# Two transformer blocks on one core: the second block's layer 0 in three column chunks instead of two

## The chip, the cores and the metric

The kernel runs on one core of a Trainium2 chip. The metric is the device time of one execution in microseconds (us), as the median of several runs. All times below are in us unless ns is written.

## What is computed

Two transformer blocks run one after the other on 512 tokens of width 1024. The change touches only the second one. It has two layers. Each works on x (512 tokens) and, in layer 0, also on a context of 256 tokens that goes through the same weights:

```
h  = layer_norm(x) * (1 + sc1) + sh1          # modulate; the context has its own sh, sc, g
y  = mixing_sublayer(h, hc, ...)              # projections by w_in, three kinds of heads, w_o
x  = layer_norm(ALPHA * x + g1 * y) * ln1_g + ln1_b
x  = layer_norm(ALPHA * x + g2 * swiglu_2(modulate(x, sh2, sc2), w_ffn_in, w_ffn_out)) * ln2_g + ln2_b
```

`swiglu_2(h)` is `(silu(h @ a) * (h @ b)) @ w_ffn_out`. In layer 1 the context is only read for keys and values (projection units 16 and 17), and has no output.

## The kernel before, in words

All activations lie transposed: eight tiles X[j] of 128 features (partitions) by 768 columns, of which columns 0 to 511 are x and 512 to 767 the context. A weight is fetched in units of 128 output features (up to 1024 k-values a row, 512 KB). `wunit` (L279) loads a unit on SP's queue two to three units ahead (`wload`, L252) and splits it (`wsplit`, L261): ScalarE rounds it to `whi` (L269), VectorE takes the difference `wlo` (L271). Activations are split in the same way, `ah` and `al`. `linear` (L305) then issues three matmuls for every k-step and chunk of columns (`mm3`, L296: lines L300, L301, L303). A unit that serves several stretches of columns at different times is fetched and split again each time.

Layer 0 of the second block (`layer2`, L1193) ends in two stages that go part by part through the columns. `PARTS` (L41) lists the parts: (first column, width).

- **"wo" stage.** `wo` (L1209) multiplies the merged heads by w_o and adds into X. For part 0, five of eight units run as filling work beside the attention (k-steps 3 to 7), then three more units, then k-steps 0 to 2 of all eight. For each later part all eight units run with all eight k-steps. A group norm with its split, ("a", part), must be done before a part begins. After each part its norm work is queued: `norms1` (L1260) is a `postln` (L1167) and then a `modulate` (L1150), two layer norms in a row, a double norm below.
- **Feed-forward** (`ffn`, L487). Unit pairs f = 0 to 21, each with two input units. The first NSKEW = 4 pairs go part by part (skewed), so that they can begin when the first part's norm is done; the middle goes over all columns; of the last group NTAIL = 4 pairs and the eight output units (21 matmuls of a chunk, 448 KB) go part by part again. After the output units of a part `norms2` (L1280) is queued: postln, then the next layer's modulate into new tiles H3, then the spill of X.

Queued norm work (`later`, L201) is a list of Python generators, first in, first out. `pump` (L213) steps through it as matmul columns are issued: a step for each 2400 x pace columns. The pace is PN for norms1 and PL for norms2, and at most 0.5 while more than one generator waits. A double norm has some 60 steps. `need` (L237) runs the steps that are left before the work that depends on them. This sets the priority of instructions; a planner (the tile framework) orders each engine's instructions by it and by readiness, except GpSimd's (POOL), which keep the order of the program.

A layer norm (`ln`, L1103): POOL adds pairs of X tiles (L1125), TensorE averages them (L1131), VectorE subtracts the mean (L1136), ScalarE squares (L1137), POOL adds squares (L441), TensorE sums over features (L369), VectorE forms 1/sqrt (`rsqrt`) and a diagonal (L394), and TensorE broadcasts it (L407). Then postln scales (L1173, L1174), or modulate writes `ah` (L1162) and `al` (L1163). Pair sums, squares and modulate's intermediate take buffers of `sqtile`, three of them.

Activation tiles come from `hilo` (L483), eight buffers for `ah` and eight for `al`. The merged heads A and the feed-forward's input H2 are the same tiles; H3 is a new set of eight from the same buffers.

Layer 1 begins with `gqa` (L1530): its `run` (L1587) goes through projection units in an order that SKEW gives. Before, SKEW[1] takes units 16, 17, 11, 12, 9, 10 over columns 0 to 383, then over 384 to 767; units other than 16 and 17 stop at column 512, so they have 128 columns left in the second chunk. `run` waits for the norms of the parts (`hparts`) that overlap a chunk. After that, units 13, 14 and 15 fill the beginning of the attention.

Layer 1's own end uses two parts of 256 columns in both kernels, with six skewed pairs.

Of the kernel before, what the change touches and what calls it, by code (L numbers as in the profile page):

```python
# [37 lines left out]

PARTS = ((0, 384), (384, 384))  # L41
SKEW = (
    (((16, 17, 11, 12, 9, 10), ((0, 256), (512, 256)), ((256, 256),)),),
    (((16, 17, 11, 12, 9, 10), ((0, 384),), ((384, 384),)),),
)
NSKEW = (3, 4, 4, 6)
NTAIL = (0, 0, 4, 0)
# [18 lines left out]
LOOK = (1, 1)  # L66


PL = ((0.8, 0.6), (0.5, 0.5))
PN = ((0.5, 0.4), (0.5, 0.5))  # L70
PF = (0.5, 0.5)
PM = (0.5, 0.5)
P2 = (0.7, 0.7)
# [56 lines left out]
class Kern:  # L130
# [1062 lines left out]
    def layer2(self, l, H, skew):  # L1193
# [4 lines left out]
        T = S if last else T2  # L1198
        parts = ((0, 256), (256, 256)) if last else PARTS
        pool = lambda name, **kw: tc.tile_pool(name=f"{name}{l}", bufs=1, reuse_waits="tile", **kw)  # L1200
# [17 lines left out]
        with pool("o") as op:  # L1218
# [41 lines left out]
            def norms1(c0, n):  # L1260
                yield from self.postln(X, c0, n, f"ln1g{l}", f"ln1b{l}")
                yield from self.modulate(X, H2, c0, n, m, 3, 4)
# [6 lines left out]
            for h in range(len(parts)):  # L1269
                self.need(("a", h))  # L1270
                for _ in wo(range(KD), h, 0, 3 if h < nw else 8):
                    pass
                self.later(("n", h), norms1(*parts[h]), PN[l][h])
            self.need(("a", len(parts) - 1))
# [5 lines left out]
        def norms2(c0, n, cnt):  # L1280
            yield from self.postln(X, c0, n, f"ln2g{l}", f"ln2b{l}", cnt)
            if last:
                for j in range(KD):
                    nc.sync.dma_start(out=self.out[j][:, c0:c0 + n], in_=X[j][:, c0:c0 + n])
                return
            if not H3:
                H3.extend(self.hilo(T2))
            yield from self.modulate(X, H3, c0, n, self.mod[1], 0, 1)
            self.spill(X, c0, n)

        def after(h, cnt):
            self.later(("l", h), norms2(*parts[h], cnt), PL[l][h])

# [769 lines left out]
```

## Time and profile before

| what | us |
|---|---|
| median of 3 runs (lowest, highest) | 3386.17 (3385.2, 3391.33) |
| the profiled execution | 3387.66 |
| its span, first to last instruction | 3385.9 |
| TensorE matmul busy in it | 3223.0 (95%) |
| VectorE busy | 2076.3 (61%) |
| ScalarE busy | 1321.3 (39%) |
| GpSimd busy | 491.3 (15%) |

PE is TensorE's matmuls, PEld its weight loads, DVE VectorE, ACT ScalarE, POOL GpSimd, SP the queue that issues the weight loads. Matmuls overlap one another, so the time of one record is longer than the pace at which they follow; the pace is a window divided by its matmuls. PEclk is the granted TensorE clock, 1.0 for 2.4 GHz and 0.5 for 1.2 GHz. A wait is put down to the instruction that ended it.

### The profile page before, as it was taken

What the parts mean: (1) busy time and instruction counts of PE and PEld (TensorE: products, weight loads), DVE (VectorE), ACT (ScalarE), POOL (GpSimd) and SP (SyncE); (2) the same over time, 40 slices, a digit from 0 to 9 for tenths busy, and PEclk for the clock granted to TensorE, in tenths of its full rate; (3) what the DMA queues carried; (4) which work ended last, traced back from release to release, by engine and by line L of the source; (5) the groups of instructions that cost most, each with busy time, mean ns of one, the idle gap of its engine ahead of it and who ended that gap; (6) DMA issues with size and microseconds to landing.
All of it is one profiled execution on the core that took longest, in us unless ns stands there. A gap on an engine that the chain in (4) does not pass through costs nothing. (4 is left out here: it accounts for less than half of the span.)

```text
span 3385.9 us, 50242 instructions
## 1 busy us (share of the span) xinstructions
PE 3223.0 (95%) x19680; PEld 2875.9 (85%) x19680; DVE 2076.3 (61%) x4419; ACT 1321.3 (39%) x2273; POOL 491.3 (15%) x462
## 2 busy tenths in 40 slices
PE   8999999999999999999898989999999899889998
PEld 7999979988888987889787878888898787888887
DVE  7993568876633769856676764222257586773335
ACT  4222346653323423234464543111135365552223
POOL 0000023333200100012212240000013212320001
PEclk9999999999999999999999999999999799999999
DMA  6663431122223556644001322221234201343233
GB/s 208 210 213 95 123 97 45 54 70 64 66 94 101 191 177 192 216 123 143 19 27 53 92 75 90 66 63 56 69 118 136 74 27 53 118 126 112 89 98 107
DMA packets 112461, 351.22 MB, mean 104 GB/s; under 512 B 12960, under 2 KB 26912, under 8 KB 111968
## 3 DMA queue, kind: packets, MB, share of 16 engines
q1 hardware_dynamic: 86464, 280.07, 26.7%
q10 hardware_dynamic: 25472, 65.84, 6.1%
q8 instruction: 155, 2.54, 0.3%
q0 software_dynamic: 288, 2.10, 0.2%
q14 instruction: 82, 0.67, 0.1%
HBM read 339.57 MB, written 8.39 MB: 103 GB/s over the span
## 5 line engine op out<-in xcount | busy, mean ns | idle before, releaser
L269 ACT ACTIVATE whi<-raw 128x1024 fp32r<-128x1024 f32 (+3 forms) x543 | 549.6, 1012 | 1439.4 <-PE mm L301 773.3
L300 PE MATMUL mm<-ah,whi 128*128 128x512 f32 (+3 forms) x2496 | 811.3, 331 | 13.0 <-ACT s L546 7.0
L301 PE MATMUL mm<-al,whi 128*128 128x512 f32 (+3 forms) x2496 | 788.1, 327 | 0.9 <-DVE al L1163 0.3
L271 DVE TENSOR_TENSOR wlo<-raw,whi 128x1024 fp32r<-128x1024 f32 (+2 forms) x464 | 558.9, 1207 | 355.7 <-ACT whi L269 352.2
L303 PE MATMUL mm<-ah,wlo 128*128 128x512 f32 (+3 forms) x2496 | 717.5, 329 | 2.8 <-DVE wlo L271 2.7
L300 PEld LDWEIGHTS mm<-ah,whi 128*128 128x128 f32 x2496 | 476.1, 191 | 65.6 <-ACT s L546 8.0
L301 PEld LDWEIGHTS mm<-al,whi 128*128 128x128 f32 x2496 | 475.7, 191 | 42.0 <-DVE al L1163 2.7
L300 PE MATMUL at<-ah,whi 128*128 128x512 f32 (+4 forms) x1368 | 479.3, 352 | 8.6 <-ACT whi L269 2.6
L301 PE MATMUL at<-al,whi 128*128 128x512 f32 (+4 forms) x1368 | 459.3, 337 | 0.1
L303 PE MATMUL at<-ah,wlo 128*128 128x512 f32 (+4 forms) x1368 | 457.7, 336 | 0.0
L303 PEld LDWEIGHTS mm<-ah,wlo 128*128 128x128 f32 x2496 | 431.0, 191 | 30.3 <-DVE wlo L271 3.8
L300 PE MATMUL mm<-gh,whi 128*128 128x256 f32 (+3 forms) x1168 | 377.0, 327 | 1.9 <-ACT gh L322 1.8
L301 PE MATMUL mm<-gl,whi 128*128 128x256 f32 (+3 forms) x1168 | 367.3, 323 | 0.7 <-DVE gl L323 0.7
L303 PE MATMUL mm<-gh,wlo 128*128 128x256 f32 (+3 forms) x1168 | 339.5, 324 | 0.3 <-DVE wlo L271 0.3
L300 PEld LDWEIGHTS at<-ah,whi 128*128 128x128 f32 x1368 | 265.0, 194 | 34.3 <-issue 5.3
L301 PEld LDWEIGHTS at<-al,whi 128*128 128x128 f32 x1368 | 266.0, 194 | 23.5 <-issue 3.3
L303 PEld LDWEIGHTS at<-ah,wlo 128*128 128x128 f32 x1368 | 265.2, 194 | 21.5 <-issue 0.5
L1125 POOL TENSOR_TENSOR sq<-x,x 128x256 f32<-128x256 f32 (+1 forms) x68 | 72.3, 1075 | 1214.7 <-DVE x L1182 809.5
L300 PEld LDWEIGHTS mm<-gh,whi 128*128 128x128 f32 x1168 | 220.9, 189 | 24.1 <-ACT gh L322 2.0
L301 PEld LDWEIGHTS mm<-gl,whi 128*128 128x128 f32 x1168 | 221.1, 189 | 18.0 <-DVE gl L323 1.4
L271 POOL TENSOR_TENSOR wlo<-raw,whi 128x1024 fp32r<-128x1024 f32 (+1 forms) x79 | 181.7, 2307 | 315.2 <-ACT whi L269 315.0
L550 DVE TENSOR_TENSOR s<-s,mm 128x256 f32<-128x256 f32 (+3 forms) x142 | 71.9, 525 | 244.3 <-PE mm L303 243.4
(396 smaller groups left out, 4787.7 us busy)
## 6 DMA issues: line engine op xcount, KB each, us to landing
raw<-in_wfin SPq DMA_DIRECT2D x116, 512.0 KB, 3.5
raw<-in_win SPq DMA_DIRECT2D x115, 512.0 KB, 3.6
wm<-in_wmod ACTq DMA_DIRECT2D x96, 512.0 KB, 4.2
raw<-in_w2in SPq DMA_DIRECT2D x52, 512.0 KB, 4.3
raw<-in_w1in SPq DMA_DIRECT2D x50, 512.0 KB, 4.2
raw<-in_wfout SPq DMA_DIRECT2D x48, 448.0 KB, 3.3
raw<-in_w1out SPq DMA_DIRECT2D x24, 448.0 KB, 3.3
raw<-in_w2out SPq DMA_DIRECT2D x24, 448.0 KB, 3.4
```

Source lines behind the costliest of these rows:

```text
L269: self.nc.scalar.activation(hi, raw, AF.Copy)
L271: eng.tensor_tensor(lo, raw, hi.bitcast(F32), op=ALU.subtract)
L300: t.matmul(ps, wh, xh, start=start, stop=False)
L301: t.matmul(ps, wh, xl, start=False, stop=False)
L303: t.matmul(ps, wl, xh, start=False, stop=stop)
L550: nc.vector.tensor_tensor(s[:, c], s[:, c], ps[1][:, 512 * b:512 * b + n], op=ALU.mult)
L1125: nc.gpsimd.tensor_tensor(x, X[j][:, c], X[j + 1][:, c], op=ALU.add)
```

## The change

The constant PARTS goes from two parts of 384 columns to three of 256: x, x, context. Layer 0's "wo" stage, its skewed first pairs and its split last pairs and output units then go through three parts. SKEW[1] becomes two entries: the six units over columns 0 to 255 and 256 to 511, then units 16 and 17 over 512 to 767. PL and PN get a value for each of the three parts. Nothing else changes.

```
-PARTS = ((0, 384), (384, 384))
+PARTS = ((0, 256), (256, 256), (512, 256))
 SKEW = (
     (((16, 17, 11, 12, 9, 10), ((0, 256), (512, 256)), ((256, 256),)),),
-    (((16, 17, 11, 12, 9, 10), ((0, 384),), ((384, 384),)),),
+    (((16, 17, 11, 12, 9, 10), ((0, 256),), ((256, 256),)), ((16, 17), ((512, 256),))),
 )
-PL = ((0.8, 0.6), (0.5, 0.5))
-PN = ((0.5, 0.4), (0.5, 0.5))
+PL = ((0.8, 0.7, 0.6), (0.5, 0.5))
+PN = ((0.5, 0.5, 0.4), (0.5, 0.5))
```

## Rows read from the trace of the kernel before

**Rows 1.** The page: engine shares, and the granted clock in 40 slices.

```profile
PE 3223.0 (95%) x19680; PEld 2875.9 (85%) x19680; DVE 2076.3 (61%) x4419; ACT 1321.3 (39%) x2273; POOL 491.3 (15%) x462
...
PEclk9999999999999999999999999999999799999999
```

**Rows 2.** Windows: layer 0's "wo" part 0, part 1, skewed pairs part 0, part 1.

```profile
core 0: us, PE busy (x) PEld busy (x) DVE busy (x) ACT busy (x) POOL busy (x), PEclk, DMA share, GB/s
1905.70:1934.50 28.80, 26.20 (x138) 24.07 (x137) 21.62 (x40) 9.52 (x18) 9.65 (x26) 0.94 0.32 94
1934.50:1985.60 51.10, 45.67 (x236) 40.85 (x234) 35.34 (x72) 21.80 (x35) 20.06 (x17) 0.97 0.34 112
1985.60:2046.90 61.30, 51.08 (x237) 44.20 (x238) 42.57 (x83) 29.27 (x52) 25.91 (x20) 0.89 0.21 68
2046.90:2086.60 39.70, 38.25 (x193) 35.94 (x192) 21.86 (x41) 16.40 (x28) 0.00 (x0) 0.91 0.32 101
```

**Rows 3.** Windows: split last pairs part 0, part 1; layer 1's projections, first and second chunk.

```profile
2447.40:2510.60 63.20, 63.20 (x362) 63.20 (x361) 31.09 (x34) 20.03 (x25) 3.04 (x3) 1.00 0.39 118
2510.60:2584.60 74.00, 73.68 (x408) 69.91 (x408) 53.87 (x99) 35.30 (x56) 21.20 (x19) 1.00 0.39 121
2584.60:2645.50 60.90, 48.65 (x241) 43.24 (x240) 41.06 (x90) 31.57 (x57) 22.50 (x22) 0.86 0.37 117
2645.50:2664.70 19.20, 19.18 (x103) 19.19 (x104) 6.45 (x15) 4.97 (x9) 2.36 (x1) 0.58 0.39 116
```

**Rows 4.** Windows: layer 1's "wo" part 0, part 1, skewed pairs part 0, part 1.

```profile
2907.00:2930.00 23.00, 18.01 (x131) 17.14 (x131) 16.07 (x38) 8.72 (x20) 9.39 (x26) 0.93 0.35 110
2930.00:2972.70 42.70, 31.88 (x229) 29.54 (x229) 31.81 (x69) 19.74 (x37) 16.87 (x17) 0.92 0.44 142
2972.70:3022.30 49.60, 45.32 (x333) 43.02 (x334) 38.76 (x90) 30.09 (x59) 18.58 (x20) 0.97 0.34 107
3022.30:3058.00 35.70, 34.71 (x282) 33.96 (x282) 22.32 (x31) 17.01 (x28) 0.00 (x0) 1.00 0.58 178
```

**Rows 5.** Windows without norms: six units at 384 columns, ten at 256.

```profile
2455.48:2480.76 25.28, 25.28 (x145) 25.28 (x145) 10.15 (x12) 8.52 (x12) 0.00 (x0) 1.00 0.38 115
3026.11:3055.02 28.91, 28.91 (x241) 28.91 (x242) 17.51 (x22) 13.48 (x20) 0.00 (x0) 1.00 0.66 200
```

**Rows 6.** Timeline of PE (start, duration): second broadcasts of the double norms, one stall.

```profile
1983.21 0.91 PE L407 MATMUL at<-dg,ones 128*128 128x384 f32 x2
...
2042.89 0.81 PE L407 MATMUL at<-dg,ones 128*128 128x384 f32 x2
...
2622.99 1.44 PE L369 MATMUL at<-ones,sq 128*128 128x1 f32 x6 [4.22 <-POOL sq L441]
...
2631.11 1.65 PE L407 MATMUL at<-dg,ones 128*128 128x384 f32 x2 [2.42 <-DVE dg L394]
...
2970.28 1.22 PE L407 MATMUL at<-dg,ones 128*128 128x256 f32 x2 [2.28 <-DVE dg L394]
...
3016.36 0.70 PE L407 MATMUL at<-dg,ones 128*128 128x256 f32 x2
```

**Rows 7.** Groups of VectorE: weight differences at 1930 to 2052 and 3026 to 3061.

```profile
L271 DVE TENSOR_TENSOR wlo<-raw,whi 128x1024 fp32r<-128x1024 f32 x18 | 26.4, 1468 | 3.0 <-ACT whi L269 2.5
...
L271 DVE TENSOR_TENSOR wlo<-raw,whi 128x1024 fp32r<-128x1024 f32 x14 | 17.1, 1224 | 10.5 <-ACT whi L269 10.5
```

**Rows 8.** Timeline of ACT: modulate's writes, layer 0's first, layer 1's first and last.

```profile
2569.35 1.30 ACT L1162 ACTIVATE ah<-sq,mod 128x384 fp32r<-128x384 f32 x2
...
3018.20 0.51 ACT L1162 ACTIVATE ah<-sq,mod 128x256 fp32r<-128x256 f32 x1 [1.86 <-DVE sq L1159]
...
3024.62 0.51 ACT L1162 ACTIVATE ah<-sq,mod 128x256 fp32r<-128x256 f32 x1 [0.64 <-DVE sq L1159]
```

**Rows 9.** Timeline of POOL: first pair sum of layer 1's second double norm.

```profile
2976.60 1.44 POOL L1125 TENSOR_TENSOR sq<-x,x 128x256 f32<-128x256 f32 x2 [9.67 <-DVE al L1163]
```

## The prediction

> **What bounds the kernel now.** I read the page first: TensorE is busy for 95% of the span, and its granted clock stays at full speed nearly everywhere [rows 1]. So time can come only from stretches where TensorE waits or runs at half clock. The change touches two of these. The first, from "wo" part 0 to the end of the skewed first units of layer 0's feed-forward, takes 180.9 us; in it the clock falls to 0.89 and 0.91 [rows 2]. The second, from the split last units of that feed-forward to the end of layer 1's first projections, takes 217.3 us; its last two windows have clocks 0.86 and 0.58 [rows 3]. Next I read layer 1's "wo" and first units, which already go by two chunks of 256 columns: that is the nearest picture of what layer 0 will look like [rows 4]. Two windows without any norm give the undisturbed pace [rows 5]: 144 matmuls of 384 columns in 25.28 us, 175.6 ns each, and 240 of 256 columns in 28.91 us, 120.5 ns each (the counts there hold one straddling matmul). Last I followed one mark: the second broadcast of each double norm (postln, then modulate), after which its outputs are written [rows 6]. In the touched stretches the waits stand at the norms' own small matmuls, for example 4.22 us for a POOL sum and 2.42 us for VectorE's diagonal [rows 6]. So a chain of norms sets the pace, and TensorE's own work is second.
>
> **TensorE's work.** Per k-step and pass, two matmuls of 384 columns become three of 256. "wo" and the feed-forward have 384 + 384 + 720 = 1488 of the former, hence 2232 of the latter: 2232 x 0.1205 - 1488 x 0.1756 = +7.7 us [rows 5]. Layer 1's first projections have 192 of 384 and 96 of 128 columns, and get 336 of 256: 40.5 us against 33.7 plus about 5.8 (an estimate, half the 256-column pace), +1 us; bounds 0 and +2. All of this is hidden as long as the norms' chain is longer, as it is below.
>
> The Trainium skill, "TensorE: Matmul & The Clock Gate", Back-to-back issue gap, gives N / 2.4 + 2.5 ns; by it three small matmuls cost 2.6 ns more than two large ones and the first sum would be +1.9 us. The rows differ from it: three at 120.5 against two at 175.6 is 10 ns.
>
> **What is added and covered.** A weight unit is fetched and split once per part, so 8 units of "wo", 8 + 8 of the feed-forward's input, 8 of its output and 2 in layer 1 come on top: 34 loads on SP's queue, 34 roundings on ScalarE, 34 differences on VectorE. The loads cost nothing: at 256 columns a stretch ran at 200 GB/s with TensorE busy throughout [rows 5]; only loads queue behind them on SP. Uncovered, a load would stall a 2.9 us unit. The 34 differences are VectorE work of 1.22 us each without POOL beside them and 1.47 with it [rows 7]; they lie beside the norms, and their price is in the norm times taken from layer 1, which has the same splits. Residual and modulate instructions do not grow: today's second part holds 128 x-columns and 256 context columns and is already issued as two, so three per row either way. The postln, mean and square instructions grow from two to three; so do the POOL sums and small rsqrt steps; they too are in layer 1's norm times. Spills go from 16 to 24 on ScalarE's queue, each behind its norm, with no one waiting but the next layer's Q tiles, a unit later: nothing.
>
> **First stretch, step by step.** "wo" part 0 takes 23.0 us in layer 1 and 28.8 now [rows 2, 4]. The five units of it in the attention's fill are 75 matmuls shorter by 55 ns, at most 4.1 us; I take 3. From the end of part 0 to the first second-broadcast: 2970.3 - 2930.0 = 40.3 us at 256 columns against 1983.2 - 1934.5 = 48.7 now. From one double norm to the next: 3016.4 - 2970.3 = 46.1 against 2042.9 - 1983.2 = 59.7 [rows 2, 4, 6]. The norms go one after the other (their queue is first in, first out and they share three scratch buffers), so three of them are 40.3 + 2 x 46.1 = 132.5 us. A third group-norm piece stands in that queue ahead of the first norm: bounds 0 and 8, I take 3. After the last broadcast the outputs take until 3025.1, 8.8 us [rows 6, 8]; the first unit follows them and seven more are 7 x 24 x 0.1205 = 20.2: 29 us, with 1 for the clock 30. Sum: -3 + 23 + 132.5 + 3 + 30 = 185.5 against 180.9, **+4.6 us**. Below: if two norms are apart by 40.3 only, -7. TensorE needs 92.5 us for the 32 units inside those 132, so it isn't the bound.
>
> **Second stretch.** Part 0 of the split units, no norm beside it: 360 x 0.1205 = 43.4. Part 1, with most of the first norm: the norm adds 74.0 - 63.2 = 10.8 us now and 49.6 - 12 x 2.89 = 14.9 in layer 1 [rows 3, 4]; I take 10, so 53 (bounds 51 and 58). Then comes the step that the change's words hide. The next layer's input H3 uses the same eight buffers as H2, which the input units read, and the planner hands a tile's buffer on only when every access to its last holder is over, whatever the columns. Now H2 is done before the norm of part 0 writes: the first write is at 2569.35, after the last input unit [rows 8]. With three parts, part 2's input units still read H2, so the outputs of part 0's norm, and behind them (they hold the scratch buffers) the norm of part 1, wait for part 2's eight input units, 23.1 us. From there two more norms follow each other: counted from a broadcast 1.8 us before the first write, and the first write 2.9 us before these units end, 46.1 - 4.7 = 41.4 to part 1's broadcast, 46.1 to the context's, 8.8 for its outputs with unit 16 behind them, 2.9 for unit 17, 2 for a half clock: 101. (Next norm's first POOL step is 6.3 us after a broadcast [rows 6, 9]; that is inside the 46.1.) Behind lie 20 us of output units and 12 projection units of 34.7, so TensorE idles some 20 us; of what follows, two units of 512 columns at most can be drawn in, 0 to 11 us; I take 3. Sum: 43.4 + 53 + 23.1 + 101 - 3 = 217.5 against 217.3, **+0.2 us**. So the gain in cover that three parts offer (12 units beside the context's norm instead of 6 beside the second part's) goes to that buffer. K's statistics come later than now, beside the projections of units 13 to 15: 0 to 4 us, I take 0.
>
> **The total** is +4.8 us on the profiled execution of 3387.66 us (span 3385.9), 3392.5; that execution lay 1.5 us over the median of the runs shown, so **3391 us**. A measurement of this kernel tells about 0.2% (6.8 us) from no change.
>
> **Rival, faster (0.25).** The outputs of part 0 do not wait, by the planner's choice or because pacing puts them earlier. Then the first two norms run beside parts 1 and 2 of 53 us each, and the context's starts 6.3 us after them: 43.4 + 106 + 6.3 + 39.8 + 8.8 + 4.9 - 3 = 206, -11 us [rows 3, 6, 9]; with the first stretch between +4.6 and -7 this gives 3368 to 3380, near 3376. For it: 9 of 12 projection units then cover the context's norm. Against it: nothing in the trace shows two holders of one buffer at once.
>
> **Rival, slower (0.27).** VectorE becomes the bound of the first stretch. A unit takes 17.51 / 10 = 1.75 us of it, and a double norm (31.8 + 38.8 - 20 x 1.75) / 2 = 17.8 [rows 4, 5]. From part 1 of "wo" to the last norm there are 32 units and three norms, 56 + 53 + 3 for the group-norm = 112 us in my 135: 83%, where layer 1 reached 78% at best and layer 0 reaches 69% [rows 2, 4]. It decides from there: if VectorE cannot be kept busier than 74%, 112 / 0.74 = 151, +16, and part 1 of the second stretch likewise +3: 3410 us. For it: each split met by a POOL sum already takes 1.47 instead of 1.22 us [rows 7]. The Trainium skill, "SBUF — State Buffer", SBUF: two separate sides, calls the port that these two share an exclusive lock for a whole instruction; by it, 24 more splits could each wait out a POOL sum of some 0.7 us, 17 us. The measured mean adds only 0.24 us.
>
> **Chances and range.** The forecast's case has 0.48, and its own range is 3380 to 3398: in it 0.36 same, 0.10 slower, 0.02 faster. The faster rival gives 0.23 faster and 0.02 same, the slower 0.24 slower and 0.03 same. Faster 0.25, same 0.41, slower 0.34. From the rivals' times the range is 3375 to 3409.
>
> **What would show it.** Right: second broadcasts of part widths 256 about 46 us apart in the first stretch; no modulate output of part 0 (L1162) before part 2's last input unit; an idle TensorE before the context's units 16 and 17; no 128-column matmuls at half clock. Wrong: outputs of part 0 beside part 2's input units, or waits on the weight splits (L271) in place of POOL sums, or a norm period far from 46 us. The sum hangs most on that period, which enters four times.

## The result, and the profile after

The changed kernel takes 3423.15 us, median of 4 runs (3410.59 to 3425.18), against 3385.68: the ratio is 1.0098, 95% interval 1.0083 to 1.0112. It is slower by 1%, 37 us, where I predicted +5 and gave the range up to 3409.

The page of the kernel after; the lines answer [rows 1].

```profile
PE 3218.5 (94%) x20514; PEld 2883.6 (85%) x20514; DVE 2131.9 (63%) x4568; ACT 1359.8 (40%) x2379; POOL 511.7 (15%) x514
...
PEclk9999999999999999999999999999998899999999
```

The shares hardly move, so the page does not tell where 37 us went. I cut both executions at five marks that exist in both: the end of layer 0's neighbourhood attention, the first full-width unit after the skewed ones, the end of the last full pair of the feed-forward, the first transpose of K's statistics (L1702), and the end of layer 1's neighbourhood attention. **First stretch** means from the first mark to the second, **second stretch** from the third to the fourth. Windows of before, then of after: first stretch, second stretch, the attention behind it. Columns: from:to, length, busy time (instructions) of PE, PEld, DVE, ACT, POOL, granted clock, DMA share, GB/s.

```profile
1905.90:2086.60 180.70, 161.00 (x797) 144.85 (x796) 121.20 (x232) 76.85 (x131) 55.59 (x62) 0.92 0.29 92
2447.50:2664.70 217.20, 204.61 (x1110) 195.44 (x1109) 132.47 (x237) 91.78 (x146) 49.10 (x45) 0.92 0.39 119
2664.70:2907.20 242.50, 226.41 (x1466) 195.53 (x1465) 177.31 (x397) 139.73 (x259) 52.96 (x51) 0.98 0.16 49
```

```profile
1894.00:2097.40 203.40, 170.09 (x1199) 160.59 (x1198) 146.42 (x309) 96.87 (x184) 64.96 (x94) 0.90 0.37 122
2458.30:2689.90 231.60, 206.51 (x1547) 198.66 (x1547) 157.44 (x309) 111.86 (x199) 61.55 (x66) 0.93 0.49 152
2689.90:2929.40 239.50, 223.25 (x1454) 193.39 (x1455) 180.34 (x397) 138.65 (x257) 51.20 (x50) 0.99 0.15 47
```

The first stretch grew by 22.7 us, the second by 14.4, and the attention behind gives 3.0 back; what follows it grew by 0.7. Together that is +34.8. The profiled execution of after shows only +22.9 (3410.59 against 3387.66), because its first mark comes at 1894.0 instead of 1905.9. Up to there its TensorE stood at half clock for 34.1 us in sum, that of before for 58.0; half of the difference is 11.9. The change touches these first 1.9 ms only in five units of filling work, so most of the difference is chance, and a stage has to be measured from its own beginning.

**The first stretch in after.** The windows answer [rows 2] and the first-stretch marks of [rows 6]: the rest of "wo" part 0; from its end to the second broadcast of the first double norm; to that of the second; to that of the third; to the end.

```profile
1892.27:1917.55 25.28, 20.09 (x136) 18.80 (x136) 17.53 (x40) 10.43 (x24) 7.93 (x25) 0.86 0.38 128
1917.55:1974.68 57.13, 51.58 (x376) 49.63 (x376) 41.68 (x85) 25.87 (x44) 21.38 (x30) 0.94 0.44 141
1974.68:2022.64 47.96, 37.82 (x277) 35.30 (x276) 39.06 (x82) 26.97 (x52) 19.54 (x20) 0.95 0.41 132
2022.64:2068.46 45.82, 35.40 (x228) 32.61 (x228) 32.72 (x76) 22.40 (x48) 16.84 (x20) 0.84 0.26 88
2068.46:2097.60 29.14, 27.12 (x195) 26.06 (x196) 17.15 (x29) 12.99 (x23) 0.00 (x0) 0.87 0.36 116
```

I had written 23, 43.3 (40.3 + 3), 46.1, 46.1 and 30. (The first row begins 1.7 us before the first mark.) The second row is the large miss, 57.1. The timeline of after, POOL and then PE (start, duration, what, idle time before it and its releaser), shows what stands in front of the first norm:

```profile
1924.32 0.20 POOL L337 TENSOR_TENSOR rst<-rsy,vc 128x2 f32<-128x2 f32 x1 [13.57 <-DVE rsy L333]
...
1927.78 0.20 POOL L347 TENSOR_TENSOR rsy<-rsy,rst 128x2 f32<-128x2 f32 x1
1927.93 2.97 POOL L1125 TENSOR_TENSOR sq<-x,x 128x256 f32<-128x256 f32 x4
```

```profile
1936.75 0.59 PE L1131 MATMUL at<-sq,avg 128*128 128x256 f32 x2
```

L337 to L347 are the root of the third group-norm piece. They run on POOL, the one engine whose order the planner keeps, and begin only when VectorE has given them their input (L333, after 13.57 us idle). The first norm's pair sums (L1125) stand behind them: they begin 10.4 us after the last unit of "wo" part 0, and TensorE takes the sums (L1131) only at 1936.75, behind units of part 1.

**The second stretch in after.** Windows: part 1 of the split units; part 2's input units; to the second broadcasts of the second and of the third norm; to the end of layer 1's first projections. They answer [rows 3].

```profile
2501.16:2549.40 48.24, 48.24 (x392) 47.77 (x391) 35.99 (x67) 26.55 (x48) 15.51 (x17) 1.00 0.59 177
2549.42:2573.34 23.92, 23.92 (x200) 23.70 (x199) 15.69 (x30) 11.46 (x18) 0.00 (x0) 1.00 0.62 188
2573.34:2621.71 48.37, 39.79 (x268) 37.15 (x267) 33.45 (x81) 22.77 (x43) 20.46 (x23) 0.89 0.47 150
2621.71:2671.83 50.12, 38.62 (x272) 36.16 (x270) 32.82 (x73) 25.91 (x53) 18.66 (x21) 0.88 0.42 141
2671.83:2682.80 10.97, 9.78 (x49) 8.92 (x50) 6.48 (x16) 3.78 (x9) 0.00 (x0) 0.61 0.00 0
```

The timeline of after (PE, ACT, POOL, PE), which answers [rows 8, 9]:

```profile
2553.70 0.70 PE L407 MATMUL at<-dg,ones 128*128 128x256 f32 x2
...
2571.60 1.30 ACT L1162 ACTIVATE ah<-sq,mod 128x256 fp32r<-128x256 f32 x3
...
2576.52 1.41 POOL L1125 TENSOR_TENSOR sq<-x,x 128x256 f32<-128x256 f32 x2 [28.59 <-DVE al L1163]
...
2689.90 0.82 PE L1702 MATMUL mm<-c_ident,rsy 128*2 128x128 f32 x6 [2.94 <-DVE rsy L353]
```

The first norm has its broadcast at 2553.70, and its first output is written 17.9 us later, 1.7 us before part 2's input units end. The second norm's pair sums come behind that. This is the wait for H2's buffers that I had foreseen.

### The profile page after: what moved, and what is told of

It is laid out like the page before. It is cut to its first block, busy times and chain, and to the rows that moved or that the text cites. A ratio compares the mean times of both kernels' runs of the same rounds, so it can differ in the third digit from the quotient of the medians.

```text
span 3408.8 us, 52389 instructions
## 1 busy us (share of the span) xinstructions
PE 3218.5 (94%) x20514; PEld 2883.6 (85%) x20514; DVE 2131.9 (63%) x4568; ACT 1359.8 (40%) x2379; POOL 511.7 (15%) x514
## 5 line engine op out<-in xcount | busy, mean ns | idle before, releaser
L300 PE MATMUL mm<-ah,whi 128*128 128x512 f32 (+2 forms) x2624 | 830.4, 323 | 10.9 <-ACT ah L1162 4.0
L271 DVE TENSOR_TENSOR wlo<-raw,whi 128x1024 fp32r<-128x1024 f32 (+3 forms) x498 | 593.9, 1195 | 354.2 <-ACT whi L269 351.0
L301 PE MATMUL mm<-al,whi 128*128 128x512 f32 (+2 forms) x2624 | 807.2, 319 | 0.3 <-DVE al L323 0.2
L303 PE MATMUL mm<-ah,wlo 128*128 128x512 f32 (+2 forms) x2624 | 736.9, 320 | 5.1 <-DVE wlo L271 5.1
L300 PE MATMUL at<-ah,whi 128*128 128x256 f32 (+2 forms) x1448 | 490.6, 340 | 9.8 <-ACT whi L269 3.0
L301 PE MATMUL at<-al,whi 128*128 128x256 f32 (+2 forms) x1448 | 469.5, 325 | 0.1
L303 PE MATMUL at<-ah,wlo 128*128 128x256 f32 (+2 forms) x1448 | 467.1, 324 | 0.4 <-DVE wlo L271 0.4
L300 PE MATMUL mm<-gh,whi 128*128 128x512 f32 (+2 forms) x1224 | 387.9, 321 | 2.6 <-ACT gh L322 2.4
L301 PE MATMUL mm<-gl,whi 128*128 128x512 f32 (+2 forms) x1224 | 378.1, 318 | 0.8 <-DVE gl L323 0.7
L303 PE MATMUL mm<-gh,wlo 128*128 128x512 f32 (+2 forms) x1224 | 350.4, 318 | 0.0
L1125 POOL TENSOR_TENSOR sq<-x,x 128x256 f32<-128x256 f32 x84 | 79.3, 955 | 1239.6 <-DVE x L1182 778.2
```

What stands on the lines that cost most here:

```text
L271: eng.tensor_tensor(lo, raw, hi.bitcast(F32), op=ALU.subtract)
L300: t.matmul(ps, wh, xh, start=start, stop=False)
L301: t.matmul(ps, wh, xl, start=False, stop=False)
L303: t.matmul(ps, wl, xh, start=False, stop=stop)
L1125: nc.gpsimd.tensor_tensor(x, X[j][:, c], X[j + 1][:, c], op=ALU.add)
```

## Experiments

Stretches are compared by their length in the profile, totals by their medians, each against runs of the kernel before taken beside it (medians 3386.92 to 3391.54 us). The first stretch with unchanged code lasted 177.1 to 180.7 us in five executions of two-chunk kernels and 203.4 to 207.2 in three of the three-chunk one. So a difference of up to 4 us in it says nothing, and every stretch below is a single execution with that uncertainty; the second repeats within 2.5 us. The half clock has to be watched too. At it matmuls of 256 columns follow each other at 213 ns instead of 119 (after, at 1930 and 1934 us), so a us of half clock costs a stretch at most half a us. The first stretch has 27.3 us of it in before and 41.0 in after.

**Each half of the change alone.** a1_first puts three chunks into the first stretch only, a2_second into the second only.

```diff
 PARTS = ((0, 256), (256, 256), (512, 256))
+TAILS = ((0, 384), (384, 384))
...
-        self.hparts = parts
+        self.hparts = tails
```

(Left out here are the lines that pass TAILS on, and SKEW[1] and PL, which are those of before. TAILS sets the chunks of the split units, their norms and layer 1's list; a2_second has the two values exchanged.)

> Three chunks of 256 from layer 0's "wo" to the skewed first units; the split last units, their norms and layer 1's first projections keep two chunks of 384. Theory (each stretch has its own loss; the first loses 11 us because the third group-norm piece stands ahead of the first norm, the second the rest): 3396 us, +11 on the kernel before, and the first second-broadcast again about 57 us after the end of "wo" part 0. Rival (the first stretch's loss is given back behind it, and the whole loss comes from the second): 3386, no change.

> Two chunks of 384 up to the skewed first units as before; three chunks of 256 in the split last units, their norms and layer 1's first projections. Theory (outputs of part 0's norm wait for H2's last reader, the norms behind it run late): 3398 us, +12, first write of H3 about 18 us after the second broadcast of part 0's norm. Rival (this stretch comes out even, as predicted with +0.2, and all of the loss is in the first): 3386.

a1_first: 3410.18 us against 3387.25, ratio 1.0067 (1.0049 to 1.0085). a2_second: 3398.15, ratio 1.0028 (1.0016 to 1.0040). First and second stretch of a1_first, then of a2_second:

```profile
1899.60:2103.00 203.40, 170.19 (x1199) 160.68 (x1199) 146.49 (x309) 96.93 (x184) 64.98 (x94) 0.90 0.38 122
2467.70:2685.10 217.40, 204.80 (x1111) 195.65 (x1110) 132.61 (x237) 91.87 (x146) 49.12 (x45) 0.92 0.38 119
```

```profile
1900.70:2081.20 180.50, 160.18 (x797) 144.00 (x797) 120.43 (x232) 76.87 (x131) 56.56 (x62) 0.93 0.28 92
2442.10:2673.20 231.10, 206.15 (x1547) 197.76 (x1546) 157.29 (x309) 111.81 (x199) 61.24 (x66) 0.94 0.50 153
```

Each half has its own loss, 22.9 and 10.9 us by the medians, and together they are 33.8 of the 37. Both stretches repeat the lengths of after. a2_second came as the theory had it. a1_first missed both expectations: my +11 for the first stretch was read from where it ends in the profiled execution of after, whose beginning is early; from its own beginning it is 22.7.

**The third group-norm piece.** a3_gn2 is the changed kernel with two pieces of 384 columns there; a4_gn3 is the kernel before with three pieces of 256.

```diff
+GPARTS = ((0, 384), (384, 384))
...
-            for h, c in enumerate(parts):
+            for h, c in enumerate(gparts):
                 self.later(("a", h), chain(self.gnorm(l, O, 0, 3, 384, (c,)), self.osplit(O, A, 0, 3, (c,))))
...
-                self.need(("a", h))
+                self.need(*[("a", i) for i, (a, w) in enumerate(gparts) if a < sum(parts[h])])
```

> The changed kernel, with the group norm of the first three o tiles by two pieces of 384 columns as in the kernel before, and all else by three chunks. Theory (the third piece delays the first double norm): pair sums of the first norm right behind "wo" part 0, first second-broadcast some 43 us after it instead of 57, 3411 us, 12 less than the changed kernel. Rival (VectorE is the bound of the stretch, at 73 to 81% busy; a piece more or less is 8 of its instructions): 3419 to 3423.

> The kernel before with one edit: the group norm of the first three o tiles by three pieces of 256 columns instead of two of 384. Theory (a third piece in the queue delays the first norm by 8 to 14 us wherever it stands): the first norm's second broadcast 57 to 62 us after "wo" part 0 instead of 48.7, 3394 to 3399 us. But the pieces for part 1 and 2 are only needed for part 1 here. Rival (VectorE bound; it is at 69% here and has room): 3386 to 3389.

a3_gn2: 3414.82 us, ratio 1.0072 (1.0055 to 1.0089), 28 us over before instead of 37, between its two expectations. a4_gn3: 3397.93, ratio 1.0028 (1.0016 to 1.0041), 11 over before, as its theory had it. First stretch of a3_gn2 with POOL's last pair sum and PE's first-norm broadcast, then that of a4_gn3:

```profile
1906.60:2103.00 196.40, 168.86 (x1198) 157.82 (x1197) 146.40 (x300) 96.69 (x179) 65.89 (x82) 0.92 0.38 127
...
1934.05 0.96 POOL L1128 TENSOR_TENSOR sq<-x,x 128x256 f32<-128x256 f32 x1 [2.89 <-DVE x L1185]
...
1973.20 0.70 PE L409 MATMUL at<-dg,ones 128*128 128x256 f32 x2
```

```profile
1901.10:2088.20 187.10, 161.03 (x800) 145.47 (x799) 121.37 (x241) 77.76 (x136) 59.48 (x74) 0.93 0.28 89
```

The piece costs 7.0 us of the first stretch where it is taken out and 6.4 where it is put in; both are above the 4 us that say nothing. Up to 5 us of the 7.0 could be clock (41.0 us of half clock against 30.7), but none of the 6.4 (27.3 in both). In a4_gn3 the first norm's second broadcast comes 8.2 us later than in before. With two pieces the pair sums follow the residuals of part 0 (released by DVE x), and the second broadcast of the first norm comes 39.2 us after the last pair sum, 66.6 us after the attention's end instead of 80.7. So the mechanism is shown, and 14 us are won at the first norm; but the two periods behind it grow from 48.0 and 45.8 to 51.6 and 49.1 us, which takes half of it back. Without the piece 15.7 us of loss remain, where my steps give +4.6 (fill and piece left out). Those 11 us were open.

**VectorE's differences, first try.** b1_nodiff leaves out differences of the third chunk in the changed kernel, b2_twice makes those of the second chunk twice in the kernel before.

```diff
-        eng.tensor_tensor(lo, raw, hi.bitcast(F32), op=ALU.subtract)
+        if third:
+            lo = hi
+        else:
+            eng.tensor_tensor(lo, raw, hi.bitcast(F32), op=ALU.subtract)
```

> The changed kernel without VectorE's weight differences for the third chunk of the first stretch (8 units of "wo" in two halves, 8 input units); TensorE multiplies by the rounded weights in their place, so the low part of these weights is left out of the output. Loads, roundings and matmuls stay. First stretch counted from the end of layer 0's neighbourhood attention to the end of the skewed units: 180.7 us before, 203.4 changed. Rival (VectorE is the bound): some 22 us less of its work, 184 to 188 us. Theory (the third group-norm piece and the norms' own chain): 200 to 204 us.

> The kernel before, with VectorE's weight difference made twice for the second chunk's 8 units of "wo" and 8 input units of the first stretch: the same number of differences as three chunks have, and nothing else of the change. First stretch 180.7 us before. Rival (VectorE is the bound): 193 to 200 us. Theory (norms' chain, VectorE has room): 181 to 184 us.

```profile
1900.70:2101.20 200.50, 168.91 (x1199) 159.58 (x1198) 136.79 (x301) 96.76 (x184) 63.95 (x94) 0.91 0.37 124
```

```profile
1901.70:2085.20 183.50, 163.20 (x798) 145.96 (x797) 128.82 (x240) 77.09 (x131) 56.52 (x62) 0.92 0.29 90
```

Lengths 200.5 (b1_nodiff) and 183.5 us (b2_twice), as the theory without VectorE has it. But VectorE's instructions changed by 8 only (309 to 301, 232 to 240): "wo" takes its later chunks by whole units, which my edit did not count, so it reached only the 8 skewed input units. The answer of 3 us each way is within the spread, and so inconclusive.

**VectorE's differences, all of them.** e1_nodiff16 (made from a3_gn2) and e2_twice16 (made from the kernel before) do the same with the 8 units of "wo" as well. The first line is of e1_nodiff16, the rest of e2_twice16.

```diff
+        third = name in ("wo2", "wfin") and idx[0] == 0 and (name == "wo2" and self.seq[i][2:4] == (0, 8) and nth == 1 or name == "wfin" and idx[1] < 8 and nth == 2)
...
+        for _ in range(2 if second else 1):
+            eng.tensor_tensor(lo, raw, hi.bitcast(F32), op=ALU.subtract)
```

> The changed kernel with the group norm by two pieces of 384, without VectorE's weight differences for the third chunk's 8 units of "wo" and 8 skewed input units; TensorE multiplies by the rounded weights in their place, so the low part of these weights is left out. The earlier edit of this kind reached only the 8 input units: 9.6 us less of VectorE, stretch 2.9 us shorter. First stretch with all differences: 196.4 us. Theory (VectorE's added differences cost the stretch about a third of their length): 19 to 23 us less of VectorE, 188 to 191 us. Rival (they lie beside other work; the 2.9 us were the clock): 194 to 197 us. A VectorE that bounds the stretch: 175 to 180 us.

> The kernel before with VectorE's weight difference made twice for the second chunk's 8 units of "wo" and 8 skewed input units of layer 0, as many as three chunks add. The earlier edit of this kind reached only the 8 input units: 7.6 us more of VectorE, stretch 2.8 us longer. First stretch 180.7 us. Theory (a third of their length): 17 to 20 us more of VectorE, 186 to 189 us. Rival (they are hidden): 181 to 184 us. A VectorE that bounds the stretch: 197 to 201 us.

```profile
1894.60:2079.60 185.00, 165.70 (x1198) 155.95 (x1198) 126.58 (x284) 96.51 (x179) 59.35 (x82) 0.93 0.41 134
```

```profile
1902.70:2093.60 190.90, 164.61 (x799) 148.87 (x798) 138.78 (x248) 78.01 (x131) 55.93 (x62) 0.90 0.27 87
```

Taking 19.8 us of VectorE's work away (146.40 to 126.58) shortens the stretch by 11.4 us, 196.4 to 185.0 (e1_nodiff16); putting 17.6 us on it lengthens the other by 10.2, 180.7 to 190.9 (e2_twice16). So 0.58 us per us in both directions, and with the spread 0.4 to 0.8: more than a third, less than a bound. The clock can account for at most 1.7 us of the 11.4 (27.3 us of half clock against 30.7) and 5.1 of the 10.2 (37.5 against 27.3). The 0.58 is an average over places that differ. In e2_twice16 all of it comes before the first norm's second broadcast, which is 10.3 us later, and the period behind is 60.2 us against 59.7; in e1_nodiff16 the periods fall from 51.6 and 49.1 to 45.7 and 47.2. First period of a3_gn2, then of e1_nodiff16:

```profile
1973.20:2024.80 51.60, 46.33 (x341) 43.85 (x340) 41.27 (x85) 28.20 (x52) 20.52 (x20) 0.97 0.38 127
```

```profile
1958.20:2003.90 45.70, 43.99 (x344) 42.27 (x342) 35.92 (x81) 28.12 (x53) 17.86 (x20) 1.00 0.42 139
```

TensorE has as many matmuls in one as in the other, so they are not what lengthens the period. How a difference does it can be seen at the end of a3_gn2's, where VectorE forms the root of a layer norm (from L378 to the diagonal, L396):

```profile
2019.89 0.16 DVE L378 TENSOR_SCALAR vc<-at 128x2 f32<-128x2 f32 x1 [2.92 <-PE at L371]
2019.97 1.23 DVE L273 TENSOR_TENSOR wlo<-raw,whi 128x1024 fp32r<-128x1024 f32 x1
...
2022.39 1.23 DVE L273 TENSOR_TENSOR wlo<-raw,whi 128x1024 fp32r<-128x1024 f32 x1
...
2024.33 0.43 DVE L396 TENSOR_TENSOR dg<-c_ident,rsy 128x256 f32<-128x256 f32 x1
```

Two differences stand among these steps, and from the first to the last it takes 4.44 us; one period later none stands there, and it takes 1.98. With that the first stretch is accounted for: 7.0 for the piece, 11.4 for the differences, and 4.3 left, where my steps without these two say 4.6. That the last two agree so closely is luck, at 4 us of spread.

**TensorE's added matmuls.** c1_lesspe is a3_gn2 without the third pass in the later chunks of "wo".

```diff
-        for ps, xh in zip(pss, xhs):
+        for ps, xh in zip(pss, xhs) if low else ():
             t.matmul(ps, wl, xh, start=False, stop=stop)
```

> The changed kernel with the group norm by two pieces of 384, without the third pass (hidden by the weights' low part) of the second and third chunk's units of "wo": 128 matmuls of 256 columns less, 15.4 us at 0.1205; the output lacks that part. The first stretch, from the end of layer 0's neighbourhood attention to the end of the skewed units, takes 196.4 us with them. Theory A (TensorE's own units push the norms' small matmuls back, so its added work counts in full): 181 to 188 us. Theory B (the norms' chain alone sets the stretch, TensorE's work is hidden as predicted): 193 to 197 us.

```profile
1898.60:2104.70 206.10, 160.11 (x1070) 148.24 (x1069) 141.84 (x300) 96.69 (x179) 61.57 (x82) 0.88 0.36 120
```

128 matmuls less, and the stretch is 9.7 us longer, outside both expectations. TensorE's idle time rises from 27.5 to 46.0 us (length minus busy time), more than the work taken away, and the granted clock falls from 0.92 to 0.88: 20.5 us more of half clock, which could account for all of the 9.7. So theory A is out, but the run doesn't isolate what TensorE's work costs, since something else changed with it: the planner also orders such a kernel anew, and a lower clock slows the norms' own matmuls; these weren't separated. That the work is hidden rests better on the two periods above: with 344 matmuls beside it e1_nodiff16's lasts 45.7 us, layer 1's with 288 lasted 46.1.

**The place of the norm's steps in the order.** d3_pace is a3_gn2 with its norms traced faster.

```diff
-PN = ((0.5, 0.5, 0.4), (0.5, 0.5))
+PN = ((0.3, 0.3, 0.3), (0.5, 0.5))
```

> The changed kernel with the group norm by two pieces of 384, and the paces of the first stretch's norms 0.3 each instead of 0.5, 0.5 and 0.4: each norm step is traced after fewer columns. First stretch 196.4 us without this. Theory (what is left over the prediction, 11 us, is where the norms' small matmuls stand in TensorE's order): 186 to 192 us. Rival (the norms' own latency): 194 to 198 us.

```profile
1904.30:2112.10 207.80, 173.81 (x1204) 161.61 (x1204) 145.55 (x301) 97.47 (x180) 61.29 (x82) 0.90 0.37 120
```

207.8 us, outside both expectations. The periods fall by 2.2 and 1.5 us (to 49.4 and 47.6), but behind the last broadcast 44.8 us remain instead of 29.1. TensorE is busy for 42.8 of them, with 341 matmuls instead of 194: units that had stood beside the norms now come behind them. So tracing the norms faster gains little on the periods and loses the cover.

**H3's buffers.** In b3_h2free part 2's input units read finished hidden tiles, so that H2 is free when part 1's end.

```diff
-                        for _ in self.linear(ps[u], w, X, ch):
+                        done = (Gl[:g1 - g0 - ntail] * 3)[:KD]
+                        for _ in self.linear(ps[u], w, done if ntail and g1 == FF and ch in hch[2:] else X, ch):
```

> The changed kernel, but the third chunk's split input units read the group's finished hidden tiles in place of H2 (same shapes and count, output not meant), so that H2's last reader is the second chunk's. Second stretch from the last full pair to K's transposes: 217.2 us before, 231.6 changed. Theory (H3's buffers are the loss): first H3 write within 2 us of the second broadcast instead of 17.9, second broadcasts of the three norms 44 to 52 us apart instead of 68 and 50, stretch 222 to 225 us, where TensorE's own work ends it. Rival (the wait is covered, the loss is in the order of units 16 and 17): 229 to 232 us.

The second stretch (the attention behind it takes 239.4 us), and second broadcast and first write of the first norm:

```profile
2469.20:2686.80 217.60, 199.81 (x1548) 192.69 (x1546) 159.03 (x309) 111.57 (x199) 61.55 (x66) 0.97 0.52 162
...
2564.92 0.70 PE L407 MATMUL at<-dg,ones 128*128 128x256 f32 x2
...
2566.91 0.91 ACT L1163 ACTIVATE ah<-sq,mod 128x256 fp32r<-128x256 f32 x2 [1.41 <-DVE sq L1160]
```

The write follows its broadcast by 2.0 us, the second broadcasts are 56.0 and 48.4 us apart instead of 68.0 and 50.1, and the stretch falls from 231.6 to 217.6, below the theory's 222. That is all of the 14 us: the wait for H2's buffers, with what comes behind it, is the second stretch's loss. Buffers of H3's own, with H2 read as it should be, were not tried.

**Filling TensorE's idle time.** b4_second13 is a2_second with layer 1's units 13 to 15 ahead of the context's 16 and 17; c4_bef13 puts these units into the two-chunk list of the kernel before.

```diff
-    (((16, 17, 11, 12, 9, 10), ((0, 256),), ((256, 256),)), ((16, 17), ((512, 256),))),
+    (((16, 17, 11, 12, 9, 10), ((0, 256),), ((256, 256),)), ((13, 14, 15), ((0, 512),)), ((16, 17), ((512, 256),))),
```

```diff
-    (((16, 17, 11, 12, 9, 10), ((0, 384),), ((384, 384),)),),
+    (((16, 17, 11, 12, 9, 10, 13, 14, 15), ((0, 384),), ((384, 384),)),),
```

> Two chunks in the first stretch, three in the second, and layer 1's units 13, 14 and 15 (one chunk of 512) put ahead of units 16 and 17 of the context's columns. Without that order it is 3398 us, 11 more than before. Theory (TensorE idles some 15 to 20 us until the context's norm is done, and these units, 16.4 us, fill it): 3384 to 3390. Rival (the attention behind loses the same units as filler and idles instead): 3396 to 3400.

> The kernel before, with layer 1's units 13, 14 and 15 in the list of skewed units, in its two chunks of 384 and 128 columns. Theory (TensorE's idle 12 us beside the second norm take them): 3380 to 3384. Rival (the attention behind misses them, and 72 matmuls of 128 columns cost some 5 us more): 3388 to 3393.

b4_second13: 3392.52 us, ratio 1.0019 (1.0006 to 1.0031), 6 better than a2_second, between the two expectations. c4_bef13: 3399.16, ratio 1.0036 (1.0024 to 1.0048), slower than both expectations. One window of c4_bef13, with the second chunk of its units:

```profile
2651.00:2695.40 44.40, 43.75 (x197) 42.15 (x197) 13.87 (x28) 11.25 (x18) 5.96 (x5) 0.50 0.30 96
```

The matmuls of 128 columns (168 instead of 96) fill the window up to 2687, and the clock is 0.50 in all of it, although TensorE idles for only 0.65 us. My "some 5 us more" was too low.

**Other widths.** c2_xc takes chunks of 512 and 256 in the second stretch with units 13 to 15 ahead; d1_first512 takes them in the first stretch alone, d2_both512 in both. The edit of c2_xc, against b4_second13:

```diff
-TAILS = ((0, 256), (256, 256), (512, 256))
+TAILS = ((0, 512), (512, 256))
...
-    (((16, 17, 11, 12, 9, 10), ((0, 256),), ((256, 256),)), ((13, 14, 15), ((0, 512),)), ((16, 17), ((512, 256),))),
+    (((16, 17, 11, 12, 9, 10), ((0, 512),)), ((13, 14, 15), ((0, 512),)), ((16, 17), ((512, 256),))),
```

(PL, left out here, is that of before. d1_first512 and d2_both512 set PARTS and GPARTS to the same two chunks.)

> Two chunks in the first stretch as before; the second stretch by two chunks of 512 (x) and 256 (context), layer 1's units 13 to 15 ahead of the context's units 16 and 17. H2's last reader then ends while the first norm is still in its statistics, so H3's buffers are free in time, and only a 256-column norm stands at the end, beside nine units of 512 columns. Theory: stretch to K's transposes about 221 us with 16.4 us of units 13 to 15 in it, 3377 to 3384 us. Rival (a norm of 512 columns needs a scratch buffer for every square where there are three, and runs over 90 us): 3392 to 3400.

> First stretch by two chunks of 512 and 256 (group norm's pieces too), second stretch as in the kernel before. Theory (the stretch is a series of norms, one more norm is what three chunks cost, and the last norm's width sets what is left behind it: 29 us at 256 columns, 43.7 at 384): the first norm some 5 to 10 us later, the end 15 us sooner after the last broadcast, stretch 172 to 180 us against 180.7, total 3379 to 3388. Rival (a norm of 512 columns, with a scratch buffer for each square, takes 20 us more than one of 384): stretch 188 to 195, total 3394 to 3402.

> Both stretches by two chunks of 512 and 256, layer 1's units 13 to 15 ahead of the context's 16 and 17. The second stretch alone gave 3384.6, 3 less than before. Theory: with the first stretch's -1 to -9 us 3375 to 3384. Rival as for the first stretch alone: 3391 to 3399.

c2_xc: 3384.61 us against 3387.81, ratio 0.9990 (0.9980 to 1.0000). d1_first512: 3389.13, ratio 1.0006 (0.9994 to 1.0018). Its first stretch takes 186.6 us against 180.7, but the end mark holds some of the next units: from the attention's end to the last full pair it is 540.1 against 541.6. d2_both512: 3388.74, ratio 1.0001 (0.9989 to 1.0013). c2_xc lies just above its theory, the other two between theory and rival. All three lie within what a measurement tells, and the gain of 3 us in c2_xc is no gain by that bound.

**Moving the differences.** f1_pool is c2_xc with every other difference of the first stretch on POOL.

```diff
-        eng = self.nc.gpsimd if self.wpool else self.nc.vector
+        eng = self.nc.gpsimd if self.wpool or first and i % 2 else self.nc.vector
```

> Two chunks in the first stretch as before, with every other weight difference of its units of "wo" and skewed input units on POOL instead of VectorE; second stretch by 512 and 256 columns with units 13 to 15 ahead of the context's, which gave 3384.6 us. Theory (VectorE's differences cost the norms more than half of their length): 12 to 14 fewer there, 16 to 18 us of VectorE, first stretch 169 to 173 us instead of 177 to 181, total 3375 to 3379. Rival (a difference of 2.3 us on POOL stands ahead of the norms' pair sums and costs as much): 177 to 186, total 3384 to 3392.

3387.06 us against 3391.54, ratio 0.9990 (0.9977 to 1.0003): as c2_xc. Its first stretch, and a group of POOL in it:

```profile
1906.30:2087.30 181.00, 160.76 (x798) 146.38 (x797) 113.03 (x216) 77.09 (x132) 83.45 (x79) 0.92 0.29 92
...
L275 POOL TENSOR_TENSOR wlo<-raw,whi 128x1024 fp32r<-128x1024 f32 x12 | 29.1, 2424 | 29.4 <-ACT whi L271 29.4
```

The stretch is no shorter, as the rival had it. POOL, whose sums the norms wait for, got 33 us for it: these 12 differences of 2.42 us and four short ones. VectorE lost 19.0 us of differences (41.6 to 22.6), but its busy time fell by 8.2 only (121.20 to 113.03), because other steps of it got longer beside POOL's differences. The first step of a norm's root, and the two differences of POOL beside it:

```profile
2037.90 2.34 DVE L337 TENSOR_SCALAR rsy<-vc 128x3 int32<-128x3 int32 x1
...
2035.22 4.99 POOL L275 TENSOR_TENSOR wlo<-raw,whi 128x1024 fp32r<-128x1024 f32 x2
```

The step takes 0.17 us where POOL does nothing, here 2.34, and it ends as POOL's second difference does (2040.2). So part of what VectorE was spared came back as waiting for POOL.

## Why the prediction was wrong, step by step

The prediction had +4.8 us, the stages show +34.8. Of the 30 us between, 18 lie in the first stretch and 11 in the second with the attention behind it.

- **What bounds it: right** for the first stretch, and for the second from part 2's input units on; before these TensorE is busy throughout, as its steps there have it. TensorE's added work in the first stretch doesn't lengthen a period (344 matmuls beside 45.7 us in e1_nodiff16). The Trainium skill, "TensorE: Matmul & The Clock Gate", Back-to-back issue gap, gives the formula that I quoted for a matmul by itself, and says that for small ones in a stream with weight loads it counts too little. At 256 columns the rows agree: 120.5 ns, 109 by the formula. Loads cost nothing: at 188 GB/s TensorE was busy for all of 23.92 us.
- **"The 34 differences ... their price is in the norm times taken from layer 1": wrong, 11 us.** That is what the 16 of the first stretch cost (e1_nodiff16, e2_twice16). The 46.1 us came from one period of layer 1. The groups of VectorE show what lay beside it, and beside the first period of a3_gn2:

```profile
L271 DVE TENSOR_TENSOR wlo<-raw,whi 128x1024 fp32r<-128x1024 f32 x10 | 12.8, 1279 | 0.3 <-ACT whi L269 0.2
```

```profile
L273 DVE TENSOR_TENSOR wlo<-raw,whi 128x1024 fp32r<-128x1024 f32 x13 | 17.7, 1368 | 1.2 <-ACT whi L271 1.1
```

  Ten differences in one, thirteen in the other, 4.9 us more of VectorE, and the period is 5.5 us longer. A period measured beside one load was added up beside another. The count alone doesn't set a period, though: ten stand also beside one of 52.9 us in c1_lesspe, at a granted clock of 0.87.
- **"A third group-norm piece ... bounds 0 and 8, I take 3": wrong.** It held the first norm up by 14 us, of which 7 stay at the end of the stretch (6.4 in a4_gn3). I had seen it in the queue ahead of the norm, and did not follow it to POOL, where the norm's sums stand behind its root.
- **Periods 46.1, twice:** 48.0 and 45.8, right in after, but by luck: there the late first norm had left fewer units beside them (277 and 228 matmuls, against 341 and 249 in a3_gn2, where they last 51.6 and 49.1). **The last 30:** 29.1, right. **"wo" part 0, 23.0:** 25.3.
- **The fill, -3:** not decided by this pair, where the half clock accounts for all of -11.9. Taking half of each execution's half clock off, the attention ends at 1873.4 to 1878.1 us in the eight executions with three chunks in the first stretch, and at 1876.9 to 1886.1 in the nine with two of 384; the medians are 3.6 us apart, so the 3 us are borne out as far as these values tell. They lie before the first mark and are not in the +22.7.
- **The buffers of H3: right, what came behind them: wrong.** The wait was foreseen in place and size (first write 1.7 us before the units' end, predicted 2.9) and shown by b3_h2free. The steps behind it were undersized: the second norm's broadcast 50.1 us after the first write instead of 44.3, the third's 50.1 later instead of 46.1, and nothing drawn in for the 3 us I took. Part 1 was cheaper than predicted, 48.2 against 53. Sum +7.4 to the end of the projections instead of +0.2. Here the periods' excess wasn't tested by itself, and its cause stays open.
- **K's statistics, 0 to 4, I take 0:** the transposes come 7.1 us behind the projections, 2.94 of it a wait for the root; the attention gives 3.0 back, so 4 net, the upper end.
- **The faster rival** asked for outputs that do not wait. b3_h2free is that case: 217.6 and 239.4, -2.7 us together instead of -11. TensorE was then nearly always busy between the first two norms (53.05 of 56.01 us in the window from 2564.92 to 2620.93), so its own units set that part.
- **The slower rival** named the right engine, and its sum for the first stretch came out: 112 us of VectorE in 151, measured 113.5 in 150.9 (57.13 + 47.96 + 45.82). That is luck. There is no share at which VectorE stops: in a3_gn2's first period it is busy for 41.27 of 51.60 us, 80%, where the rival's limit was 74%, and 7 us of the stretch are the third piece's. Below any such share each added us cost 0.58 on average, since the norm's steps stand among the differences in one queue (a3_gn2's root above). The exclusive port that the Trainium skill, "SBUF — State Buffer", SBUF: two separate sides, describes is seen in the traces: five of the 1024-column differences in a3_gn2's first stretch take 1.74 to 1.76 us instead of 1.21, and each ends 1.08 us behind a POOL sum. But it is not the loss: instructions of VectorE that are over 0.5 us longer than the shortest of their form add 4.3 us in that stretch and 7.3 in before's; my estimate from that page was 17.
- **The range** ended at the slower rival alone. The third piece, VectorE and the norms behind the buffer wait are no alternatives; they added up: 7 + 11 + 4 in the first stretch and 14 - 3 in the second.

## What to carry to other kernels

When a chain of small steps sets a stage and its duration is taken from another stage, count what lies beside it there on every engine that the chain passes through: here work in the same queue cost it a share of its length long before the engine was full. Follow each added background piece to the engine whose order is fixed, and see who stands behind it there. And compare two executions stage by stage, each from its own beginning.

## What the runs showed of the hardware

- The first 1.9 ms, alike in both kernels but for five units of filling work, ended 11.9 us apart in two executions, at 58.0 and 34.1 us of half clock in sum.
- With a granted clock of 1.00 and TensorE busy throughout, the same 361 us of full units take 360.9 us in some executions and 364.7 in others. Windows of 60 us in after, then in a1_first:

```profile
2157.40:2217.40 60.00, 60.00 (x344) 52.44 (x343) 17.66 (x23) 8.76 (x10) 0.00 (x0) 1.00 0.20 62
```

```profile
2163.00:2223.00 60.00, 60.00 (x342) 52.32 (x341) 16.66 (x22) 9.39 (x11) 0.00 (x0) 1.00 0.20 62
```

  There are two paces and no third: matmuls of 512 and 256 columns follow each other at 231.5 and 118.1 ns in 11 of the 19 profiled executions, and at 233.3 and 120.0 in the other 8, 1.8 to 1.9 ns more at either width. What differs, the profile doesn't show.
- 168 matmuls of 128 columns, issued nearly without a gap, ran at half clock from the first to the last, and the clock stayed at 0.50 for 44.4 us (c4_bef13); it was back at 1.00 when matmuls of 512 columns had taken their place.
- VectorE and POOL can hold each other up: a step of 0.17 us took 2.34 beside a POOL difference (f1_pool).
